# Retention outputs copied out of their PSUM bank by ScalarE, their squares summed in place, their transposes in the same bank

## The chip, the core and the metric

The kernel runs on one core of a Trainium2 chip. The core has TensorE (PE, matrix products, with a loader of its own for weights, PEld), VectorE (DVE), ScalarE (ACT), GpSimd (POOL) and SyncE (SP, which here issues DMAs); each works through its own queue in order, and they wait for each other by semaphores. PE writes into PSUM, eight banks of 2 KB per partition, which the other engines read; everything else is in SBUF. The metric is the device time of one execution in microseconds (us).

## The reference, cut to what matters

A trunk of two layers. In each, one projection of the modulated input feeds three token mixers and a gate; the mixer that the change touches is the bidirectional retention: four heads of width 64, ten chunks (tiles) of 128 tokens, eight of the latent tokens and two of the context.

```python
def step(s, inp):
    qi, ki, vi = inp
    a = jnp.einsum('bihd,bjhd->bhij', qi, ki) * intra
    o = (jnp.einsum('bhij,bjhe->bihe', a, vi)
         + jnp.einsum('bihd,bhde->bihe', qi, s) * q_dec[None, :, :, None])
    ...
def bidir_retention(q, k, v, log_g, s0_f, s0_b):
    ...
    o = rms_norm(o_f + jnp.flip(o_b, 1))   # over the 64 of each head
    return o.reshape(B, L, RET_W).astype(v.dtype), ...
# then: concat(o_ret, o_gqa, o_mla) * silu(z_gate), one output projection, residual add
```

## The kernel before

The layer's gate projection is computed output group by output group (z_blk, four calls, 24 matmuls per PSUM bank: L683 to L685, the operands split in a high and a low part; ScalarE takes a tanh, L688, VectorE multiplies it into a tile eo, L690, 256 columns each, and SP stores it, L691). Between halves of these groups z_blk takes one step of a side generator, `more` (L693), which runs in turn: key transposes, latents, the retention (retention, driver loop from L919), and last the preparation of the attention, which puts its key, value and kpr loads into SP's queue (L1086, L1101 to L1104, L1090, L1144) and their splits onto ScalarE and VectorE (L196, L197, L1147). So PE has gate matmuls to do while the short chains of the retention pass from engine to engine. The program's scheduler merges these into one fixed order per engine, by its own estimates; nothing in the code fixes it.

The retention goes over its ten tiles in a pipeline of four stages; step t of the driver loop does stage c of tile t-2, stage b of tile t-1 and stage a of tile t.

- Stage a: q is transposed (PE, L868, four) and k (L871, two) into two "tp" banks; VectorE scales q (qdT, L875), ScalarE writes q into a block-diagonal tile BD (L877, L878) and k into kT (L880); GpSimd advances a state (L825, L826). The transposes of stage d of tile t-3 are called from here and write into the free half of k's bank.
- Stage b: two products of BD and kT (PE, L893), masked by VectorE into At (L895).
- Stage c: eight matmuls (PE, L903 and L904) write the tile's output into one half of the bank "o"; ScalarE squares it into the other half (L905), VectorE sums the squares per head (L907), takes the inverse root in 13 small operations (newton, L145 to L161) and multiplies the output by it from PSUM into the SBUF tile oret (L910).
- Stage d: two transposes of oret (PE, L916) and ScalarE's copy to the mixer's result yx (L917).

Of the kind "o" there is one bank at that time, so the first L903 of a tile waits until L910 of the tile before has read it. Of the kind "acc" there are five: the gate groups and the attention's scores (L1247, L1248; maximum by VectorE, L1256; exponential with its sum by ScalarE, L1270) take turns in them. In the attention 128 queries against 512 keys are one score tile.

Of the kernel before, what the change touches and what calls it, by code (L numbers as in the profile page):

```python
# [10 lines left out]
F32 = mybir.dt.float32  # L11
F32R = mybir.dt.float32r
I32 = mybir.dt.int32
AF = mybir.ActivationFunctionType
ALU = mybir.AluOpType
AX = mybir.AxisListType
PSUM = bass.MemoryType.PSUM

P = 128
# [62 lines left out]
def hybrid_trunk(tc, I, O):  # L82
# [3 lines left out]
    V, A, G, T = nc.vector, nc.scalar, nc.gpsimd, nc.tensor  # L86
# [47 lines left out]
    def bank(tag):  # L134
        if tag == "o":
            return pp.tile([P, 512], F32, name=tag, tag=tag, bufs=1)
        if tag == "m":
            tag = "tp"
        bufs = {"acc": NACC, "tp": 7 - NACC}[tag]
        return pp.tile([P, 512], F32, name=tag, tag=tag, bufs=bufs)  # L140
# [647 lines left out]
    def retention(l, rt, load, kv):  # L788


        dec, cdec = dec_all[:, l], cdec_all[:, l]
        MT = rt.tile([P, 4, 128], F32, name="MT")
        dma(MT.rearrange("p h c -> p (h c)"), s_mt[l])
        pos = rt.tile([P, 256], F32, name="pos", tag="cur", bufs=2)[:, 0:128]
        dma(pos[0:64, :], I["rel"][0:1, 0, :].to_broadcast([64, 128]))
        dma(pos[64:128, :], I["rel"][127:128, 1, :].to_broadcast([64, 128]))

        def bc(ap, lo=0, hi=P):
            return ap.unsqueeze(2).to_broadcast([hi - lo, 4, 64])

        def h4(ap):
            return ap.rearrange("p (h d) -> p h d", h=4)

        F, B = slice(0, 64), slice(64, 128)
        S = rt.tile([P, NT, 256], F32, name="S")
        fin = rt.tile([P, 256], F32, name="fin")
        for d, t in ((F, 0), (B, NL - 1)):
            dma(h4(S[d, t, :]), I["state_ret"][0, l, d.start // 64].rearrange("h d e -> d h e"))
        V.memset(S[F, NL, :], 0.0)
        V.memset(S[B, NT - 1, :], 0.0)  # L810


        decT = rt.tile([P, 4, 128], F32, name="decT")
        for h in range(4):
            lg = lgT_all[:, l, h:h + 1]
            A.activation(decT[:, h, :], pos, AF.Exp, scale=lg, bias=lg)

        def advanced(eng, d, nxt, cur, inc=None):

            if inc is not None:  # L820
                eng.tensor_tensor(h4(nxt), h4(cur), bc(cdec[d], d.start, d.stop), op=ALU.mult)
                eng.tensor_tensor(nxt, nxt, inc, op=ALU.add)
            else:
                st = rt.tile([P, 256], F32, name="cur", tag="cur", bufs=2)[d]
                pin(eng.tensor_tensor(h4(st), h4(cur), bc(cdec[d], d.start, d.stop), op=ALU.mult))  # L825
                eng.tensor_tensor(nxt, nxt, st, op=ALU.add)  # L826

        def increments(t, kv):
            kd = rt.tile([P, 4, 2, 64], F32, name="kd", tag="kd", bufs=3)
            V.tensor_tensor(kd, h4(kv[:, 0:256]).unsqueeze(2).to_broadcast([P, 4, 2, 64]),  # L830
                            dec[:, 2:4, :].rearrange("p a h -> p h a").unsqueeze(3).to_broadcast([P, 4, 2, 64]), op=ALU.mult)
            ps = bank("m")
            for h in range(4):
                T.matmul(ps[:, h * 64:(h + 1) * 64], kd[:, h, :, :].rearrange("p a b -> p (a b)"),
                         kv[:, 256 + h * 64:256 + (h + 1) * 64], start=True, stop=True)

            if t not in (0, NL, NT - 1):
                advanced(V, B, S[B, t - 1, :], S[B, t, :], ps[B, :256])
            elif t == NL:
                advanced(V, B, fin[B, :], S[B, t, :], ps[B, :256])  # L840
            elif t == NT - 1:
                V.tensor_copy(S[B, t - 1, :], ps[B, :256])

            if t != NL - 1:
                A.copy(S[F, t + 1, :] if t != NT - 1 else fin[F, :], ps[F, :256])

        qqs = {}

        def doubled(t):
            if t < NT:  # L850
                qqs[t] = rt.tile([P, 4, 2, 64], F32, name="qq", tag="kd", bufs=3)
                pin(pool_copy(qqs[t], h4(yx[t][:, 0:256]).unsqueeze(2).to_broadcast([P, 4, 2, 64])))

        for t in range(NT - 1, -1, -1):
            yield
            nx_kv = load(t - 1) if t else load(0)
            increments(t, kv)
            if t < 2:
                doubled(1 - t)
            kv = nx_kv  # L860

        BD = rt.tile([P, 2, 256], F32, name="BD")
        V.memset(BD, 0.0)

        def stage_a(t, kv, qq):
            pt = bank("tp")
            for h in range(4):
                T.transpose(pt[:, h * 128:(h + 1) * 128], qq[:, h, :, :].rearrange("p a b -> p (a b)"), ident)  # L868
            pk = bank("tp")
            for j in range(2):  # L870
                T.transpose(pk[:, j * 128:(j + 1) * 128], kv[:, j * 128:(j + 1) * 128], ident)  # L871
            if t >= 3:
                stage_d(t - 3, outs.pop(t - 3), pk[:, 256:512])
            qdT = rt.tile([P, 4, 128], F32, name="qdT", tag="qdT", bufs=2)
            V.tensor_tensor(qdT.rearrange("p h c -> p (h c)"), pt, decT.rearrange("p h c -> p (h c)"), op=ALU.mult)  # L875
            pq = pt.rearrange("p (j x c) -> p x j c", j=2, x=2)
            A.copy(BD[0:64, :, 0:128], pq[0:64, 0])  # L877
            A.copy(BD[64:128, :, 128:256], pq[64:128, 1])  # L878
            kT = rt.tile([P, 2, 128], F32, name="kT", tag="kT", bufs=1)
            A.copy(kT.rearrange("p j c -> p (j c)"), pk[:, 0:256])  # L880

            if t < NL - 1:
                advanced(G, F, S[F, t + 1, :], S[F, t, :])
            elif t == NL:
                advanced(G, F, fin[F, :], S[F, NT - 1, :])
                for d in range(2):
                    dma(new_state[0, l, d].rearrange("h d e -> d h e"), h4(fin[64 * d:64 * d + 64, :]))
            return kv, qdT, kT

        def stage_b(kT):  # L890
            pa = bank("m")
            for j in range(2):
                T.matmul(pa[:, j * 256:(j + 1) * 256], kT[:, j, :], BD[:, j, :], start=True, stop=True)  # L893
            At = rt.tile([P, 4, 128], F32, name="At", tag="kd", bufs=3)
            V.tensor_tensor(At.rearrange("p h c -> p (h c)"), pa, MT.rearrange("p h c -> p (h c)"), op=ALU.mult)  # L895
            return At

        def stage_c(t, kv, qdT, At):
            bo = bank("o")
            po, sq = bo[:, 0:256], bo[:, 256:512]  # L900
            for h in range(4):
                hs = slice(h * 64, (h + 1) * 64)
                T.matmul(po[:, hs], At[:, h, :], kv[:, 256 + h * 64:256 + (h + 1) * 64], start=True, stop=False)  # L903
                T.matmul(po[:, hs], qdT[:, h, :], S[:, t, hs], start=False, stop=True)  # L904
            A.activation(sq, po, AF.Square)  # L905
            ss = sm.tile([P, 4], F32, name="ss4", tag="ss4")
            V.tensor_reduce(ss, h4(sq), axis=AX.X, op=ALU.add)  # L907
            rstd = newton(ss, 4, 1.0 / 64)
            o = rt.tile([P, 256], F32, name="oret", tag="cur", bufs=2)
            V.tensor_tensor(h4(o), h4(po), bc(rstd), op=ALU.mult)  # L910
            return o

        def stage_d(t, o, pt):

            for i in range(2):
                T.transpose(pt[:, i * 128:(i + 1) * 128], o[:, i * 128:(i + 1) * 128], ident)  # L916
            A.copy(yx[t][:, 0:256], pt)  # L917

        st, At, outs = {}, {}, {}  # L919
        for t in range(NT + 3):  # L920
            yield
            if 2 <= t < NT + 2:
                outs[t - 2] = stage_c(t - 2, st[t - 2][0], st[t - 2][1], At.pop(t - 2))
            if 1 <= t <= NT:
                At[t - 1] = stage_b(st[t - 1][2])
            if t < NT:
                nx_kv = load(t + 1) if t + 1 < NT else None
                if t:
                    doubled(t + 1)
                st[t] = stage_a(t, kv, qqs.pop(t))  # L930
                kv = nx_kv
            elif t >= 3:
                stage_d(t - 3, outs.pop(t - 3), bank("tp")[:, :256])

    def cache_keys(l, pool, bufs):

# [581 lines left out]
    st, p1, acts = open_p1(ws)  # L1518
# [66 lines left out]
    for l in range(DEPTH):  # L1585
        ws = Weights(out_blocks(l) + (in_blocks(l + 1) if l + 1 < DEPTH else []))
        att.run(ws)
        st, p1, acts = open_p1(ws)
# [3 lines left out]
        ss, rstd = {}, {}  # L1592
# [100 lines left out]
```

## Time and profile before

| | us |
|---|---|
| runs of the kernel | 2162.13, 2163.22, 2165.7; median 2163.22 |
| profiled execution | 2162.85 |
| its span, first to last instruction | 2161.1 |
| PE busy | 2084.2 (96%) |
| VectorE busy | 1502.0 (70%) |
| ScalarE busy | 1183.5 (55%) |
| GpSimd busy | 978.2 (45%) |
| granted TensorE clock, mean | 0.992 |

In layer 0 the retention's L910 runs from 424.6 to 486.2 us of the span and the first scores come at 506.46; in layer 1 the last L910 runs at 1528.1. The attention follows each. In a timeline a row is one run of like instructions on one engine: its start, its length, the line, the tile written and read. What is in brackets is how long the engine was idle before, and what released it. Matmuls are pipelined, so what one costs PE is the distance between two starts, not its length.

### The profile page before, as it was taken

To read this page: it belongs to the slowest core of one execution; us is meant where nothing else is said; L and a number is where in the kernel's file an instruction comes from. 1 tells how busy PE (TensorE), PEld (TensorE's weight loads), DVE (VectorE), ACT (ScalarE), POOL (GpSimd) and SP (SyncE) were. 2 spreads that over 40 slices of the span, in tenths; PEclk is the share of its full clock that TensorE was granted. 3 is DMA by queue.
4 is the path that set the end of the run, shared out by engine and by line. 5 is a ranking of instruction groups with operands and counts; after the bars stand their busy time and mean duration, and the time that the engine had idled before them with its cause. 6 is when DMAs were issued, how large, how long until landed. Compare 5 with 4: busy or idle time off the path is not lost. (4 is left out here: it accounts for less than half of the span.)

```text
span 2161.1 us, 42292 instructions
## 1 busy us (share of the span) xinstructions
PE 2084.2 (96%) x14888; PEld 1870.0 (87%) x14888; DVE 1502.0 (70%) x3830; ACT 1183.5 (55%) x3180; POOL 978.2 (45%) x1444
## 2 busy tenths in 40 slices
PE   7999999999999999999999999998999999999998
PEld 3899987788888888888999999887788888888898
DVE  4625583666889999997174358546689899999824
ACT  3503333225788888886243233322488888888623
POOL 2341242315576465533543324233375656453474
PEclk8999999999999999999999999999999999999999
DMA  9542446414111010004143212452311111000322
GB/s 315 145 145 63 123 112 204 122 49 117 36 44 28 20 30 25 13 27 136 46 153 102 66 54 55 140 152 66 109 46 30 32 30 32 14 22 18 98 91 98
DMA packets 189117, 173.30 MB, mean 80 GB/s; under 512 B 35833, under 2 KB 171625, under 8 KB 188905
## 3 DMA queue, kind: packets, MB, share of 16 engines
q1 hardware_dynamic: 187464, 165.35, 25.7%
q10 hardware_dynamic: 1440, 5.24, 0.6%
q8 instruction: 119, 1.95, 0.4%
q14 instruction: 94, 0.76, 0.1%
HBM read 124.77 MB, written 45.76 MB: 79 GB/s over the span
## 5 line engine op out<-in xcount | busy, mean ns | idle before, releaser
L256 PE MATMUL acc<-wh,ah 128*128 128x256 f32 (+1 forms) x1760 | 503.4, 286 | 1.8 <-ACT ah L404 1.8
L258 PE MATMUL acc<-wh,al 128*128 128x256 f32 (+1 forms) x1760 | 500.6, 284 | 2.5 <-DVE al L405 2.4
L257 PE MATMUL acc<-wl,ah 128*128 128x256 f32 (+1 forms) x1760 | 502.7, 286 | 0.0
L1256 DVE TENSOR_REDUCE nm<-acc 128x1 f32<-128x512 f32 (+1 forms) x624 | 411.7, 665 | 39.0 <-PE acc L1250 27.0
L1293 DVE TENSOR_TENSOR pT<-tp,pT 128x512 fp32r<-128x512 f32 (+1 forms) x624 | 413.2, 664 | 36.1 <-ACT pT L1292 30.6
L1292 ACT CAST pT<-tp 128x512 fp32r<-128x512 f32 (+1 forms) x624 | 356.5, 573 | 139.1 <-PE tp L1288 132.8
L1270 ACT ACTIVATE pn<-acc,nm 128x512 f32<-128x512 f32 (+1 forms) x624 | 421.3, 681 | 19.9 <-DVE nm L1261 17.4
L1288 PE MATMUL tp<-ident,pn 128*128 128x128 f32 x2400 | 424.1, 274 | 3.9 <-DVE pT L1293 2.4
L256 PEld LDWEIGHTS acc<-wh,ah 128*128 128x128 f32 x1760 | 334.9, 190 | 13.1 <-issue 8.2
L258 PEld LDWEIGHTS acc<-wh,al 128*128 128x128 f32 x1760 | 332.0, 189 | 5.3 <-DVE al L405 4.5
L257 PEld LDWEIGHTS acc<-wl,ah 128*128 128x128 f32 x1760 | 334.0, 190 | 0.8 <-issue 0.8
L1304 PE MATMUL o<-pT,V 128*128 128x256 f32 x1200 | 326.3, 294 | 0.7 <-DVE yx L1317 0.6
L1288 PEld LDWEIGHTS tp<-ident,pn 128*128 128x128 f32 x2400 | 287.6, 140 | 34.6 <-PE tp L1288 5.8
L1305 PE MATMUL o<-pT,V 128*128 128x256 f32 x1200 | 314.4, 284 | 0.0
L1304 PEld LDWEIGHTS o<-pT,V 128*128 128x128 f32 x1200 | 227.1, 189 | 19.2 <-DVE yx L1317 5.1
L1305 PEld LDWEIGHTS o<-pT,V 128*128 128x128 f32 x1200 | 227.2, 189 | 16.6
L192 POOL TENSOR_SCALAR wh<-raw 128x512 fp32r<-128x512 f32 (+2 forms) x144 | 82.4, 582 | 321.2 <-PE acc L258 143.2
L193 POOL TENSOR_TENSOR wl<-raw,wh 128x512 fp32r<-128x512 f32 (+2 forms) x144 | 164.7, 1155 | 5.2
L1247 PE MATMUL acc<-K,Qm 128*128 128x512 f32 (+1 forms) x312 | 140.6, 451 | 1.0
L683 PE MATMUL acc<-ah,wh 128*128 128x512 f32 (+1 forms) x384 | 141.4, 368 | 0.0
L684 PE MATMUL acc<-ah,wl 128*128 128x512 f32 (+1 forms) x384 | 139.8, 364 | 0.0
L685 PE MATMUL acc<-al,wh 128*128 128x512 f32 (+1 forms) x384 | 139.5, 363 | 0.0
(278 smaller groups left out, 3898.3 us busy)
## 6 DMA issues: line engine op xcount, KB each, us to landing
raw<-in_w_ada_dram SPq DMA_DIRECT2D x96, 256.0 KB, 3.2
raw<-in_w_in_dram SPq DMA_DIRECT2D x56, 256.0 KB, 2.9
kv<-s_rkv SPq DMA_DIRECT2D x40, 256.0 KB, 2.8
s_gT<-eo SPq DMA_DIRECT2D x80, 128.0 KB, 2.2
yx<-in_x_sample_dram SPq DMA_DIRECT2D x16, 512.0 KB, 6.4
gt<-s_gT SPq DMA_DIRECT2D x60, 128.0 KB, 2.1
raw<-in_w_in_dram SPq DMA_DIRECT2D x56, 128.0 KB, 2.5
raw<-in_w_out_dram SPq DMA_DIRECT2D x48, 128.0 KB, 3.0
```

Source lines behind the costliest of these rows:

```text
L193: G.tensor_tensor(wl, raw, wh.bitcast(F32), op=ALU.subtract)
L256: T.matmul(ps, ah[:, k, :], wh, start=(k == 0), stop=False)
L257: T.matmul(ps, ah[:, k, :], wl, start=False, stop=False)
L258: T.matmul(ps, al[:, k, :], wh, start=False, stop=(k == KC - 1))
L683: T.matmul(ps, wh, ah[:, k, :], start=(k == 0), stop=False)
L1256: V.tensor_reduce(nm[:, b:b + 1], ps, axis=AX.X, op=ALU.max, negate=True)
L1270: A.activation(pn, ps, AF.Exp, bias=p.ng[i], accum_out=p.su[:, i, b:b + 1])
L1288: T.transpose(pt[:, c * 128:(c + 1) * 128], pn[:, c * 128:(c + 1) * 128], ident)
L1292: A.copy(ph, p3)
L1293: V.tensor_tensor(pl, p3, ph.bitcast(F32), op=ALU.subtract)
L1304: T.matmul(p.po, vc, p.gran[b][:, 0, c, :], start=(ch == 0), stop=False)
L1305: T.matmul(p.po, vc, p.gran[b][:, 1, c, :], start=False, stop=(ch == last))
```

## The change

Stage c gets its bank from the driver loop. When the eight matmuls are done, ScalarE copies the output to oret at once, and then squares it head by head in place in the bank, each square writing its sum into one column of ss; newton works on ss as before, and VectorE multiplies oret by the result in place in SBUF. Stage d is called first in step t, ahead of stage c of tile t-2, and its transposes go into the other half of that step's bank "o" instead of the half of a "tp" bank; the last stage ds take no "tp" bank any more. Per layer ten reductions on VectorE go, and ten squares of 256 columns on ScalarE become ten copies and forty squares of 64 columns with sums. PE, GpSimd and SP have the same instructions as before.

```diff
@@ stage_a
-            if t >= 3:
-                stage_d(t - 3, outs.pop(t - 3), pk[:, 256:512])
...
@@ stage_c
-        def stage_c(t, kv, qdT, At):
-            bo = bank("o")
-            po, sq = bo[:, 0:256], bo[:, 256:512]
+        def stage_c(t, kv, qdT, At, po):
...
-            A.activation(sq, po, AF.Square)
+            o = rt.tile([P, 256], F32, name="oret", tag="cur", bufs=2)
+            A.copy(o, po)
             ss = sm.tile([P, 4], F32, name="ss4", tag="ss4")
-            V.tensor_reduce(ss, h4(sq), axis=AX.X, op=ALU.add)
+            for h in range(4):
+                hs = slice(h * 64, (h + 1) * 64)
+                A.activation(po[:, hs], po[:, hs], AF.Square, accum_out=ss[:, h:h + 1])
             rstd = newton(ss, 4, 1.0 / 64)
-            o = rt.tile([P, 256], F32, name="oret", tag="cur", bufs=2)
-            V.tensor_tensor(h4(o), h4(po), bc(rstd), op=ALU.mult)
+            V.tensor_tensor(h4(o), h4(o), bc(rstd), op=ALU.mult)
             return o
@@ driver loop
         for t in range(NT + 3):
             yield
+            if t >= 2:
+                bo = bank("o")
+            if t >= 3:
+                stage_d(t - 3, outs.pop(t - 3), bo[:, 256:512])
             if 2 <= t < NT + 2:
-                outs[t - 2] = stage_c(t - 2, st[t - 2][0], st[t - 2][1], At.pop(t - 2))
+                outs[t - 2] = stage_c(t - 2, st[t - 2][0], st[t - 2][1], At.pop(t - 2), bo[:, 0:256])
...
-            elif t >= 3:
-                stage_d(t - 3, outs.pop(t - 3), bank("tp")[:, :256])
```

In the changed kernel the lines are: matmuls of stage c L899 and L900, copy L902, squares L906, product L908, transposes of stage d L914, copy to yx L915; stage b L891, its product At L893, qdT L873, BD L875 and L876, kT L878.

The scheduler orders the instructions anew. PE in the loop, before; a tile's small matmuls stand close together (acc are the gate matmuls, ah and al the split operands):

```order
L893 MATMUL tp<-BD,kT 128x256 x2
L868 MATMUL tp<-ident,qq 128x128 x4
L683 MATMUL acc<-ah_129,wh 128x512
L903 MATMUL o<-kv,At 128x64
L904 MATMUL o<-S,qdT 128x64
...
L871 MATMUL tp<-ident,kv 128x128 x2
L916 MATMUL tp<-ident,oret 128x128 x2
```

PE in the loop, after; eight gate matmuls follow stage c, then come stage b and stage a, and some 21 gate matmuls stand in a step where before some 11 did:

```order
L914 MATMUL o<-ident,oret 128x128 x2
L685 MATMUL acc<-al_132,wh 128x256
L683 MATMUL acc<-ah_127,wh 128x512
L684 MATMUL acc<-ah_127,wl 128x512
L899 MATMUL o<-kv,At 128x64
L900 MATMUL o<-S,qdT 128x64
...
L685 MATMUL acc<-al_128,wh 128x512
L683 MATMUL acc<-ah_127,wh 128x512
```

The last stage d has moved from ahead of the layer's remaining gate groups to just ahead of the attention's first scores. ScalarE in the loop, after (th is the gate's tanh):

```order
L915 COPY yx<-o 128x256
L688 ACTIVATE th<-acc 128x256
L902 COPY oret<-o 128x256
L906 ACTIVATE o,ss_5830<-o 128x64 x2
L875 COPY BD<-tp 64x2x128
L906 ACTIVATE o,ss_5830<-o 128x64
L876 COPY BD<-tp 64x2x128
L906 ACTIVATE o,ss_5830<-o 128x64
L878 COPY kT<-tp 128x256
```

Three of the four squares now stand ahead of the second BD copy. PE at the end of the retention, after; behind the last stage d stand the first scores:

```order
L683 MATMUL acc<-ah_127,wh 128x512
L684 MATMUL acc<-ah_127,wl 128x512
L685 MATMUL acc<-al_128,wh 128x512
L914 MATMUL o<-ident,oret 128x128 x2
L1247 MATMUL acc<-K,Q_6422 128x512 x2
L1248 MATMUL acc<-K,Q_6422 128x512
L1247 MATMUL acc<-K,Q_6422 128x512
L683 MATMUL acc<-ah_129,wh 128x512
```

Before, 91 gate matmuls stood between the last L916 and the first L1247. SP there, before (st are the staging tiles of the loads):

```order
L691 DMA s_gT_58<-eo 128x256 x5
L1086 DMA st<-s_gkT_66 64x4x128 x3
L1086 DMA st<-s_gkT_66 64x2x128
L1101 DMA st<-in_cache_gqa_v_dram 128x4x64
L1102 DMA st<-s_kv_62 128x3x64
L1104 DMA st<-s_kv_62 128x7x64
L691 DMA s_gT_58<-eo 128x256 x2
L1090 DMA st<-s_mk_68 64x512 x3
```

SP there, after; the same loads stand behind six stores, and one store is left among them:

```order
L691 DMA s_gT_58<-eo 128x256 x6
L1086 DMA st<-s_gkT_66 64x4x128 x3
L691 DMA s_gT_58<-eo 128x256
L1086 DMA st<-s_gkT_66 64x2x128
L1101 DMA st<-in_cache_gqa_v_dram 128x4x64
L1102 DMA st<-s_kv_62 128x3x64
L1104 DMA st<-s_kv_62 128x7x64
L1090 DMA st<-s_mk_68 64x512 x3
```

VectorE there, after: the eo of the sixth store stands within the last newton, and the key splits (L197) follow the product:

```order
L159 TENSOR_TENSOR nwu<-nwu,nwx 128x4
L690 SCALAR_TENSOR_TENSOR eo<-th,acc 128x256
L160 SCALAR_TENSOR_TENSOR nwy<-nwu,nwy 128x4
L908 TENSOR_TENSOR oret<-oret,nwy 128x256
L690 SCALAR_TENSOR_TENSOR eo<-th,acc 128x256
L197 TENSOR_TENSOR K<-st,K 64x512 x3
L1256 TENSOR_REDUCE nm<-acc 128x1
```

Before, five evacuations and the first key splits alternated behind the last L910, with PE still in gate matmuls.

## Rows read from the trace of the kernel before

**Rows 1.** The page's first section: busy time, share of the span, instructions.

```profile
PE 2084.2 (96%) x14888; PEld 1870.0 (87%) x14888; DVE 1502.0 (70%) x3830; ACT 1183.5 (55%) x3180; POOL 978.2 (45%) x1444
```

**Rows 2.** Line L910 (last two: who waited, line waited at, us, times).

```profile
L910 DVE TENSOR_TENSOR oret<-o,nwy x20: 407/425/425, 424.6 to 1528.1; 128x256 f32<-128x256 f32 x20
...
  PE o L903: 9.3, 11
```

**Rows 3.** PE's timeline, layer 0: start, length, operation, [idle before <- releaser].

```profile
436.29 0.40 PE L683 MATMUL acc<-ah,wh 128*128 128x512 f32 x1
436.53 0.40 PE L684 MATMUL acc<-ah,wl 128*128 128x512 f32 x1
...
439.76 0.43 PE L903 MATMUL o<-kv,At 128*128 128x64 f32 x2 [1.07 <-DVE oret L910]
...
446.17 1.02 PE L893 MATMUL tp<-BD,kT 128*128 128x256 f32 x4
447.02 0.33 PE L903 MATMUL o<-kv,At 128*128 128x64 f32 x2
...
448.76 0.61 PE L868 MATMUL tp<-ident,qq 128*128 128x128 f32 x4
449.20 0.38 PE L871 MATMUL tp<-ident,kv 128*128 128x128 f32 x2
```

**Rows 4.** ScalarE's timeline, the same tiles.

```profile
449.02 0.37 ACT L905 ACTIVATE o<-o 128x256 f32<-128x256 f32 x1 [1.40 <-PE o L904]
...
471.55 0.37 ACT L877 COPY BD<-tp 64x256 f32<-64x256 f32 x1 [1.81 <-DVE nwu L151]
471.82 0.37 ACT L917 COPY yx<-tp 128x256 f32<-128x256 f32 x1
472.20 0.37 ACT L878 COPY BD<-tp 64x256 f32<-64x256 f32 x1
```

**Rows 5.** ScalarE's groups by form at L358: total and mean ns.

```profile
L358 ACT ACTIVATION_READ_ACCUMULATOR e<-acc 128x1 f32 x40 | 8.1, 202 | 0.0
...
L358 ACT ACTIVATE e<-acc 128x128 f32<-128x128 f32 x20 | 5.8, 288 | 0.0
```

**Rows 6.** VectorE's timeline, two tiles.

```profile
477.94 0.59 DVE L152 TENSOR_SCALAR nwy<-nwu 128x4 int32<-128x4 int32 x1
...
483.83 0.17 DVE L150 TENSOR_SCALAR nwx<-ss 128x4 f32<-128x4 f32 x1
...
486.21 0.42 DVE L910 TENSOR_TENSOR oret<-o,nwy 128x256 f32<-128x256 f32 x1
```

**Rows 7.** GpSimd's timeline behind the last tiles.

```profile
476.93 1.57 POOL L1171 TENSOR_TENSOR Q<-yx,Q 64x256 fp32r<-64x256 f32 x2
```

**Rows 8.** SP's queue, its loads for the attention: length is of all x.

```profile
488.20 4.81 SPq L1086 DMA_DIRECT2D st<-s_gkT  x4
...
501.52 8.96 SPq L1144 DMA_DIRECT2D st<-s_kpT  x16
```

**Rows 9.** ScalarE's timeline at the start of the attention.

```profile
491.07 0.62 ACT L196 CAST K<-st 64x512 fp32r<-64x512 f32 x1 [2.36 <-DMA st<-s_gkT]
...
513.97 0.40 ACT L1147 CAST kpr<-st 128x256 fp32r<-128x256 f32 x1
...
516.82 0.68 ACT L1270 ACTIVATE pn<-acc,nm 128x512 f32<-128x512 f32 x1
...
517.49 0.69 ACT L1270 ACTIVATE pn<-acc,nm 128x512 f32<-128x512 f32 x1
```

**Rows 10.** PE's timeline, the first and the fourth score tile.

```profile
506.46 0.86 PE L1247 MATMUL acc<-K,Q 128*128 128x512 f32 x3
...
517.16 0.47 PE L1247 MATMUL acc<-K,Q 128*128 128x512 f32 x1 [0.71 <-DVE eo L690]
```

**Rows 11.** The same stretch of layers 0 and 1: us, busy of engines, PEclk, DMA.

```profile
439.76:517.16 77.40, 74.22 (x431) 64.59 (x432) 46.91 (x152) 24.83 (x63) 17.89 (x28) 0.96 0.28 79
1482.17:1557.96 75.79, 71.60 (x431) 61.75 (x432) 46.59 (x152) 24.81 (x63) 17.95 (x28) 1.00 0.28 81
```

## The prediction

> **What bounds the kernel now.** I read the page's first section, then the waits of one line, then the timelines of one layer. TensorE (PE) is busy for 96% of the span [rows 1]: a change counts only where it makes PE wait or lets it stop waiting. So the question for the line that is replaced (L910, the product that reads the PSUM bank "o" last) is who waited for it: PE's first L903 of a tile, 9.3 us in 11 of the 20 tiles of both layers [rows 2]; PE's timeline shows one, 1.07 us before 439.76 [rows 3]. Those 9.3 us are all that an earlier copy can give back.
>
> The rest of the argument needs prices. PE goes from one 512-column matmul of the gate projection to the next in 0.235 us; the eight small matmuls of stage c take 1.74 (447.02 to 448.76), stage b 0.85 (446.17 to 447.02), the four transposes of q 0.44 (448.76 to 449.20) and so the two of k some 0.22 [rows 3]. On ScalarE the 256-column square begins 0.26 after PE has gone on from stage c (448.76, 449.02) and lasts 0.37; copies follow each other after 0.27 (64 partitions) and 0.38 [rows 3, 4]. On VectorE newton and L910 take 2.8 (483.83 to 486.21, plus 0.42), and each of newton's 13 operations waits for the one before [rows 6].
>
> **The change, part by part; per layer, ten tiles.**
>
> (1) *Removed: the wait for L910.* The bank is now read last by the fourth square, before newton begins. -9.3 / 2 = -4.65.
>
> (2) *Added on ScalarE: a copy and four squares with sums in place of one square.* A square of 64 columns is not in the trace. The nearest rows are 0.37 for 256 columns [rows 4] and 0.29 for 128 with its sum, whose read-out is 0.20 more [rows 5]: 64 columns give about 0.24. Of two exponentials one behind the other, the second starts 0.67 after the first, which lasts 0.68 itself [rows 9], so there the read-out costs nothing: a square costs 0.24 at the least and 0.44 at the most; I take 0.3. VectorE loses the reduction L907, 0.4 per tile, off PE's path.
>
> (3) *Moved: the loop's order.* After, a tile's chain stands in this order on PE: two transposes of the output (stage d), 3 gate matmuls, stage c, 8 gate matmuls, stage b, q's transposes, 2, k's transposes, 8, and the next stage d. That gives two places where PE may wait, in about 7 steady tiles.
> A hand-over between engines I set at 0.06, an estimate: newton's 13 operations of 0.17 fill 2.38 [rows 6], so one within VectorE is some 0.02, and I take three of these. Stage b needs both BD copies, and ScalarE now does the copy and three of the squares ahead of the second: 0.26 + 0.38 + 3 x 0.3 + 0.27 + 0.38 + 0.06 = 2.25 after stage c, against a cover of 8 x 0.235 = 1.88. Wait 0.37, with a square at 0.24 or 0.44 0.2 or 0.8: 7 x 0.37 = **2.6** (1.4 to 5.6).
> Stage d needs newton, which begins after the fourth square: 0.26 + 0.38 + 1.2 + 0.65 + 0.06, newton and product 2.8, and in between on VectorE the masked product At (512 columns from PSUM, so between L910's 0.42 and twice that: 0.6), and 0.06: 6.0. Each gate evacuation (eo, 256 columns from PSUM as L910, 0.42) that falls in it adds 0.4, none to two, 0.3 on average; a VectorE operation stretched beside GpSimd (L152 0.59 instead of 0.17 while L1171 runs) adds 0.4 [rows 6, 7], half of the time. So 6.5, against 18 x 0.235 + 0.85 + 0.44 + 0.22 + 0.37 (the wait before b) = 6.1. Wait 0.4: 7 x 0.4 = **2.8** (0 to 4).
> Stage c follows d after 3 matmuls and needs the yx copy, since d and c share the bank: 0.26 + 0.38 + 0.06 against 0.14 + 0.70, so nothing (at most 0.1 each). Before, d wrote into the half of k's bank that was free, and its copy kept nobody waiting.
> The multiply's input is now SBUF twice (L908), where L910 had one in PSUM and took 407 to 425 ns in all 20 tiles [rows 2]; I price it the same. The Trainium skill, "SBUF — State Buffer", section "Who interferes with whom", says that a VectorE instruction with two SBUF inputs contends with a GpSimd instruction that reads SBUF, and that the loser blocks. By that rule L908 can lose what the stretched row shows, 0.42 in each of 20 tiles: up to 8.4 more, 2202; it stands beside the worse rival and not in the sum.
>
> (4) *The last tile.* Behind the last stage c the program now has 13 gate matmuls, 3.05, and then the last stage d; nothing else is left of the layer's retention to fill in. Its chain: 0.26 + 0.38 + 1.2 + 0.06 + 2.8 + 0.4 (an eo that now stands within that newton) + 0.06 = 5.2, so a wait of 2.1 (1.8 to 2.7), and more if GpSimd's q pieces (L1169, L1171), which ran right behind the last tiles before, stretch two to five of the small operations by 0.42 each: 0.9 to 2.1. I take **3.7** (1.8 to 4.8).
>
> (5) *The attention's first keys.* Before, SP issued the key loads (L1086) at 488.20 and PE came to the first score matmul at 506.46, 18 us later, without a wait [rows 8, 10]. After, those loads stand in SP's queue behind the store of the eo that lies in the last newton, about 0.2 us before PE's last d, and the score matmuls stand right behind d. From issue to the cast on ScalarE 2.87, the cast 0.62 and a subtraction on VectorE of about its size: 4.2 [rows 8, 9]; less 0.34 for d and the head start, less some slack in the estimate: **3.7** (3.2 to 4.2).
>
> (6) *The sixth score tile.* There are five "acc" banks; the sixth tile needs one that an exponential has freed, and the first exponential stands on ScalarE behind the four kpr casts, the last of 27 loads on SP. Counted from the first load's issue: 16 kpr loads took 8.96, 0.56 each [rows 8], so 27 without a stop are 15.1; landing up to 2.9, cast 0.4, exponential 0.6: 19.0 at the least. Before, with stores and their waits in between, the last kpr load was out at 510.48, 22.3 after the first: 26.2 at the most. The order after has one store among the 27 where before had four, but the casts have to keep their buffers free: 22.5. PE gets there after 4.2, ten score matmuls and 24 gate matmuls at 0.235 and 24 of half width: 4.2 + 8.0 + 2.9 + 0.7 (its present wait for an eo at the fourth tile, 517.16 [rows 10]) = 15.8. Wait **6.7** (3.2 to 10.4). Before, the same casts were done at 514.37 and the exponentials could begin when the scores came (516.82) [rows 9].
>
> *Sum per layer:* -4.65 + 2.6 + 2.8 + 3.7 + 3.7 + 6.7 = 14.85; two layers 29.7. *The clock:* layer 0's granted clock was 0.96 over its retention and layer 1's 1.00; the same stretch was 1.6 longer in layer 0 [rows 11]. With longer waits I expect about the same loss in each layer, 3.0 in all instead of 1.6: +1.4 (-1.6 to +3). The profiled run took 2162.85; 2162.85 + 31.1 = 2194.0, and the median of the runs is 0.4 above it, which is inside the rounding: 2194.
>
> **Rivals.**
> *Faster.* Only (1) comes true: stage b and d are covered, the key loads are out at least 10 us before the last d because the scheduler's queue order leaves SP free, and the clock stays up: -9.3 - 1.6, 2152. For it: the bank really is released some 3 us earlier. Against: the order of the rows shows the score matmuls behind d and the loads behind that eo; SP cannot pass the store. Chance 0.05.
> *Same.* The delay is given back in the attention, where PE would then wait less for exponentials: 2163. Against: PE is 96% busy over the span, with few gaps to take it up [rows 1], and the stages behind start when PE gets to them. Chance 0.04.
> *Worse than forecast.* In steps b and d the high ends hold: squares at 0.44 and VectorE blocked by GpSimd in every tile (0.42 for L908 or a newton step): +3.0 and +2.9 per layer, and the sixth tile late by another 4. 2194 + 2 x 9.9 = 2214. For it: the 0.59 of L152 in the row; against: only a few of newton's operations are stretched now. The rule of the page that I named would add to this. Chance 0.11.
> *The forecast*, 0.80.
>
> **How the numbers follow.** Low ends of every term: -4.65 + 1.4 + 0 + 1.8 + 3.2 + 3.2 = 4.95 per layer, 9.9, less 1.6 of the clock: 2171. High ends: -4.65 + 5.6 + 4 + 4.8 + 4.2 + 10.4 = 24.4, 48.7, plus 3: 2214.5. Not all ends come at once, so 2172 to 2214 holds the forecast's case and half of the worse one; the faster and the same case lie outside. A measurement of this kernel can tell 0.2%, 4.3 us, from no change. Faster by more 0.05, within 0.04, slower 0.91.
>
> **What would show it.** In the changed kernel's waits of PE: none for the output's copy or squares at the first matmul of stage c beyond 0.1; L891 waiting for ScalarE's BD copies and L914 for L908, both below 1 us in the steady tiles; L914 of the last tile 2 us or more; the first L1247 behind a DMA or the K subtraction 3 to 4 us, and a later L1247 behind an exponential 3 to 10 us, in both layers alike. In ScalarE's timeline a square with its read-out of 0.24 to 0.44. I am wrong if those two waits at the start of the attention are small (the loads were early after all), or if they are there and the stretch from there to the layer's end is shorter by as much.

## The result and the profile after

The changed kernel takes 2210.78 us (median of four runs, 2207.81 to 2212.83), the kernel before 2162.68 beside it: a ratio of 1.0219, 95% interval 1.0201 to 1.0236, slower by 48 us. The forecast was 2194, range 2172 to 2214: slower as forecast and inside the range, 17 us above its middle. The profiled execution took 2211.14.

The page of the changed kernel, its busy times; they answer to [rows 1]:

```profile
PE 2102.7 (95%) x14888; PEld 1875.6 (85%) x14888; DVE 1489.5 (67%) x3810; ACT 1209.1 (55%) x3340; POOL 976.2 (44%) x1444
```

PE has the same 14888 instructions and is busy for 18.5 us more (2102.7 against 2084.2). The waits of PE in the whole execution (us in total, times, longest), first of the kernel after, then two of the kernel before:

```profile
PE tp L1358 <- POOL rb L1355: 16.1, 6, 5.1
PE acc L1247 <- ACT pn L1270: 11.7, 2, 6.0
PE o L914 <- DVE oret L908: 11.0, 14, 3.4
PE acc L1247 <- DVE K L197: 8.0, 4, 3.8
...
PE tp L891 <- ACT BD L876: 2.0, 11, 0.4
```

```profile
PE tp L1358 <- POOL rb L1355: 9.9, 6, 3.2
...
PE acc L1247 <- ACT pn L1270: 1.3, 2, 0.7
```

The wait of [rows 2], 9.3 us at the first matmul of stage c, is gone from the list: the change did what it says. In its place stand L914, stage d behind newton, 11.0; the first keys, 8.0; the sixth score tile behind its exponential, 11.7 where there were 1.3; and L1358, a transposition in the attention behind GpSimd, 16.1 where there were 9.9. What changed is 10.4 + 10.7 (L916, stage d before, waited 0.3) + 8.0 + 1.7 (stage b before 0.3) + 6.2 - 9.3 = 27.7 of the 48.3 us between the two spans (2209.4 and 2161.1).

The end of layer 0's retention on PE, after; it answers to [rows 3, 10]:

```profile
508.74 0.41 PE L914 MATMUL o<-ident,oret 128*128 128x128 f32 x2 [3.44 <-DVE oret L908]
512.90 0.77 PE L1247 MATMUL acc<-K,Q 128*128 128x512 f32 x1 [3.75 <-DVE K L197]
...
515.39 0.63 PE L683 MATMUL acc<-ah,wh 128*128 128x512 f32 x1
515.82 0.63 PE L684 MATMUL acc<-ah,wl 128*128 128x512 f32 x1
...
532.59 0.79 PE L1247 MATMUL acc<-K,Q 128*128 128x512 f32 x1 [5.74 <-ACT pn L1270]
```

All three waits stand where they were looked for: 3.44 for the last newton, 3.75 for the first key, 5.74 at the sixth tile. Between them PE goes from one gate matmul to the next in 0.43 (515.39 to 515.82), where it took 0.235 in [rows 3]. The same is seen in the granted clock (the number ahead of the last two), columns as in [rows 11]:

```profile
510.00:520.00 10.00, 6.82 (x21) 5.18 (x22) 6.20 (x11) 3.98 (x7) 3.04 (x5) 0.66 0.44 116
530.00:540.00 10.00, 6.71 (x25) 4.96 (x26) 6.10 (x14) 6.96 (x18) 5.37 (x8) 0.66 0.64 171
580.00:590.00 10.00, 6.36 (x31) 5.96 (x32) 3.28 (x7) 2.53 (x8) 8.04 (x14) 0.66 0.03 7
```

A mean of 0.66 in 10 us is some 6.8 us at half speed, the lower of the two levels, 1.2 GHz. In the kernel before the same stretches stood at 1.00; 440 to 450 was one of two in layer 0's retention that stood lower, at 0.83, half as long:

```profile
440.00:450.00 10.00, 10.00 (x63) 9.04 (x63) 6.34 (x22) 2.89 (x9) 2.03 (x4) 0.83 0.19 44
```

Not all of this time is work. After the change the clock is at half speed from 510.1 on, while PE still waits for the first key, and the part behind 512.90 alone slows matmuls (the first busy time is PE's):

```profile
510.10:512.90 2.80, 0.00 (x0) 0.03 (x1) 0.97 (x2) 1.49 (x3) 2.50 (x5) 0.50 0.55 168
512.90:516.90 4.00, 3.72 (x8) 2.64 (x9) 2.70 (x4) 0.84 (x3) 0.44 (x1) 0.50 0.43 101
```

Over the whole execution the mean granted clock fell from 0.992 to 0.984:

```profile
core 0: 2209.4 us, clock 0.984
```

(1 - 0.984) x 2209.4 is 35.4 us of full speed not granted, (1 - 0.992) x 2161.1 is 17.3: 18 us more, part of which fell on time in which PE waited anyway. In all stretches at half speed together PE was busy for 51.4 us after the change and for 26.6 before; half of that, 25.7 and 13.3 us, is what the slow clock cost its work: 12.4 us more. So the 48.3 us are 29.8 of idle time (27.7 of them the waits above) and 18.5 of busy time, 12.4 of these the clock. Of the other 6, most is time that the list of waits leaves out, as (3) shows further down.

Further rows of after. ScalarE's first two squares in the last tile, and SP's queue at the start of the attention; they answer to [rows 4, 5] and to [rows 8]:

```profile
502.67 0.21 ACT L906 ACTIVATE o<-o 128x64 f32<-128x64 f32 x1
...
503.02 0.21 ACT L906 ACTIVATE o<-o 128x64 f32<-128x64 f32 x1
```

```profile
487.69 20.64 SPq L691 DMA_DIRECT2D s_gT<-eo  x6
508.39 2.00 SPq L1086 DMA_DIRECT2D st<-s_gkT  x3
...
522.65 7.45 SPq L1144 DMA_DIRECT2D st<-s_kpT  x16
```

A square of 64 columns lasts 0.21, and the next begins 0.35 after the first has begun. SP waits in its six stores from 487.69 on and issues the first key load at 508.39, 0.35 ahead of the last stage d.

### The profile page after: what moved, and what is told of

Its sections match the earlier page's. It is cut to its first block, busy times and chain, and to the rows that moved or that the text cites. A ratio compares the mean times of both kernels' runs of the same rounds, so it can differ in the third digit from the quotient of the medians.

```text
span 2209.4 us, 42399 instructions
## 1 busy us (share of the span) xinstructions
PE 2102.7 (95%) x14888; PEld 1875.6 (85%) x14888; DVE 1489.5 (67%) x3810; ACT 1209.1 (55%) x3340; POOL 976.2 (44%) x1444
## 4 chain that ended last, share of the span: by engine, by line
PE 66%; DVE 5%; POOL 4%; ACT 4%; issue 2%; DMA 2%; SPq 0%; POOLq 0%; DVEq 0%; ACTq 0%
PE tp L1288 11%; PE o L1304 6%; PE acc L1247 6%; PE acc L257 6%; PE acc L258 6%; PE acc L256 6%; PE o L1305 6%; PE acc L1248 5%; PE acc L1250 3%; PE acc L685 2%; PE acc L683 2%; PE acc L684 2%; ACT o L906 1%; PE o L900 1%; PE o L899 1%
## 5 line engine op out<-in xcount | busy, mean ns | idle before, releaser
L1247 PE MATMUL acc<-K,Qm 128*128 128x512 f32 (+1 forms) x312 | 141.2, 453 | 1.0
L1248 PE MATMUL acc<-K,Qm 128*128 128x512 f32 (+1 forms) x312 | 139.7, 448 | 0.0
```

The costliest lines, as they stand in the source:

```text
L1247: T.matmul(ps, p.Q[:, 0, qs], K, start=True, stop=False)
L1248: T.matmul(ps, p.Q[:, 1, qs], K, start=False, stop=not p.mla)
```

## Experiments: the order of stage c and stage d

Theory 1 was formed from the order of the rows. In the changed kernel stage d of a tile stands on PE ahead of stage c of the next, and d waits for its tile's newton. So copy, squares, newton, product, d, the yx copy and c make one chain from tile to tile, and that the bank is released early is of no use. In this kernel only ScalarE and VectorE read PSUM, and after the change ScalarE alone reads the output's half of the bank. Theory 2 was that ScalarE's and VectorE's new work is the cause, theory 3 that the shared bank is.

**e1: stage c first, then stage d.**

```diff
             if t >= 2:
                 bo = bank("o")
-            if t >= 3:
-                stage_d(t - 3, outs.pop(t - 3), bo[:, 256:512])
             if 2 <= t < NT + 2:
                 outs[t - 2] = stage_c(t - 2, ..., bo[:, 0:256])
+            if t >= 3:
+                stage_d(t - 3, outs.pop(t - 3), bo[:, 256:512])
```

> The changed kernel with one thing swapped: in a step of the loop the eight matmuls of stage c come first and the transposes of stage d behind them, still in the same bank. Theory 1 (the order d before c is the cause: c of one tile stands on PE behind d of the tile before, which waits for that tile's newton, so copy, squares, newton, d and the yx copy form one chain from tile to tile, the retention takes 21 gate matmuls per step, ends late and leaves nothing between the last d and the scores): the steps shrink to some 14 gate matmuls, PE waits for nothing longer than 1 us at the scores, 2150 to 2165. Theory 2 (what ScalarE and VectorE got, the copy, forty squares and a product with two SBUF inputs, is the cause): hardly better than the changed kernel, 2195 to 2211. Theory 3 (the shared bank is the cause): 2195 to 2211 as well, since it is still shared.

Measured: 2155.92, ratio to the kernel before 0.9962 (0.9947 to 0.9977). In the profile of e1 PE does not wait for the bank at stage c, the waits for the first keys are gone, and the rest is as before the change:

```profile
PE tp L1358 <- POOL rb L1355: 9.6, 6, 3.1
...
PE acc L1247 <- DVE eo L690: 1.8, 2, 1.0
...
PE o L914 <- DVE oret L908: 1.0, 2, 0.5
```

From one L914 to the next it takes 6.7 us (445.85 to 452.53) where the changed kernel takes 9.1 (444.55 to 453.62), and 41 + 24 + 24 gate matmuls stand between the last d and the scores, where the changed kernel has none: what fills its longer steps is missing there. First e1, then the changed kernel:

```profile
445.85 0.44 PE L914 MATMUL o<-ident,oret 128*128 128x128 f32 x2
...
452.53 0.44 PE L914 MATMUL o<-ident,oret 128*128 128x128 f32 x2
```

```profile
444.55 0.41 PE L914 MATMUL o<-ident,oret 128*128 128x128 f32 x2 [0.26 <-DVE oret L908]
...
453.62 0.41 PE L914 MATMUL o<-ident,oret 128*128 128x128 f32 x2 [0.24 <-DVE oret L908]
```

Even with its longer steps the changed kernel waits for the product at d, so the chain really takes that long. Two lines in another order are worth 55 us. Everything that theories 2 and 3 blame is still in e1.

**e2: the copy at once, stage d where it was before.**

```diff
-            if t >= 2:
-                bo = bank("o")
-            if t >= 3:
-                stage_d(t - 3, outs.pop(t - 3), bo[:, 256:512])
...
+            # in stage_a, as before
+            if t >= 3:
+                stage_d(t - 3, outs.pop(t - 3), pk[:, 256:512])
```

> Only the first half of the change: the copy at once, the squares in place and the product in SBUF; stage d is where it was before, in k's bank. Theory 1 (order) : the waits of stage c for the product go (9.3 us in the profile of the kernel before) and nothing comes late, 2150 to 2160. Theory 2 (ScalarE's and VectorE's new work): 2195 to 2211. Theory 3 (shared bank): 2150 to 2160, and 30 us or more below e1.

Measured: 2154.91, ratio 0.9962 (0.9949 to 0.9975), the same as e1. So the shared bank costs nothing where c comes first, with squares of this length (e10 below doubles them), and the first half of the change alone is a gain of some 8 us, which is about what [rows 2] showed as the wait for L910.

**e3: the kernel before, only stage d moved to the start of the step.**

```diff
             yield
+            if t >= 3:
+                stage_d(t - 3, outs.pop(t - 3), bank("tp")[:, :256])
             if 2 <= t < NT + 2:
                 outs[t - 2] = stage_c(t - 2, st[t - 2][0], st[t - 2][1], At.pop(t - 2))
```

> The kernel before, with its one square, reduction and product from PSUM, where only stage d is moved to the start of a step, ahead of stage c, into a bank of its own of the kind tp. Theory 1 (order): stage c stands behind d, d behind newton; the steps become some 18 gate matmuls long and PE waits for L910 at d instead of at c; some slack is left behind the last d (13 gate matmuls of 512, 24 of 256, 24 of 512 columns), so the scores are not late: 2160 to 2180. Theories 2 and 3: as the kernel before, 2161 to 2165.

Measured: 2170.91, ratio 1.0038 (1.0023 to 1.0053): slower than before by 8, as theory 1 has it, without any of the new work of ScalarE. PE waits for the product at d now, and at the scores for an evacuation:

```profile
PE acc L1245 <- DVE eo L690: 9.9, 2, 5.0
...
PE tp L914 <- DVE oret L908: 6.1, 13, 0.9
```

**e4: the changed kernel with one square and one reduction.**

```diff
-            for h in range(4):
-                hs = slice(h * 64, (h + 1) * 64)
-                A.activation(po[:, hs], po[:, hs], AF.Square, accum_out=ss[:, h:h + 1])
+            A.activation(po, po, AF.Square)
+            V.tensor_reduce(ss, h4(po), axis=AX.X, op=ALU.add)
```

> The changed kernel with one square of 256 columns in place and one reduction on VectorE instead of four squares with sums. Theory 1 (order): the chain from tile to tile is still there but some 0.6 us shorter per tile, the last d stands 23 gate matmuls ahead of the scores, so the key loads are out earlier: 2165 to 2195. Theory 2 in the narrow form (the four squares with their read-outs are the cause): 2150 to 2165.

Measured: 2190.13, ratio 1.0123 (1.0106 to 1.014). The chain is still there and shorter: 8.3 from one L913 (stage d here) to the next, where the changed kernel takes 9.1. The last d of layer 0 comes at 498.08 instead of 508.74. That is worth 21 us of the 48: the last d now has 23 gate matmuls behind it, the first key comes in time, and of the three waits at the end only that of the sixth tile is left.

```profile
PE acc L1246 <- ACT pn L1269: 13.7, 2, 6.9
```

So the length of the chain counts, but because of the order.

## Experiments: the waits at the attention and the clock

**e5: PE kept at work in two of the waits.**

```diff
+            if t == NT + 2:
+                for _ in range(30):
+                    T.transpose(bo[:, 0:128], ident, ident)
             if t >= 3:
                 stage_d(t - 3, outs.pop(t - 3), bo[:, 256:512])
+            if t == NT + 2:
+                for _ in range(28):
+                    T.transpose(bo[:, 0:128], ident, ident)
```

> The changed kernel with 30 transposes of the identity, which nobody reads, on PE ahead of each layer's last stage d and 28 behind it, into the free half of that bank: 3.3 and 3.1 us of work in place of the two waits of 3.4 and 4.0 us, so that PE is not idle there. Theory A (the time behind is set by the loads on SP, through the kpr casts and the first exponential): the half-clock stretch behind the first scores goes, but the 2 us that it cost come back as a longer wait of the sixth score tile: 2206 to 2213. Theory B (each wait carries the price of the slow clock behind it, which adds to the total): some 4 to 7 us less, 2203 to 2207.

Measured: 2203.99, ratio 1.0193 (1.0174 to 1.0211), 6.8 less than the changed kernel by the medians, though PE does 116 transposes more. The two did not run side by side, and the intervals of their ratios overlap a little (1.0201 to 1.0236). The two waits are gone from PE's list. The sixth tile and the clock:

```profile
PE acc L1253 <- ACT pn L1276: 14.8, 2, 7.6
```

```profile
510.92 0.39 PE L1253 MATMUL acc<-K,Q 128*128 128x512 f32 x1
511.15 0.40 PE L1254 MATMUL acc<-K,Q 128*128 128x512 f32 x1
```

```profile
core 0: 2202.2 us, clock 0.987
```

The first scores now go 0.23 apart (510.92, 511.15) instead of 0.42 to 0.6 in the changed kernel, and the sixth tile waits 1.6 us longer per layer, as theory A had it; but the total fell as theory B had it. By the mean clocks, (1 - 0.987) x 2202.2 = 28.6 us not granted against 35.4, so 6.8 less. PE's busy time shows it too: 2108.9 us, some 2096.3 without the transposes (3.34 and 2.98 per layer), against 2102.7, so 6.4 less. That is the size of the gain; it isn't proof, since the last d also came 2.2 us earlier in layer 0 (506.49 against 508.74), 0.9 of it in the loop.

**e6: four kpr loads instead of sixteen.**

```diff
-                for j in range(4):
-                    dma(st[32 * j:32 * j + 32, :n].rearrange("p (t c) -> p t c", c=P), src[...])
+                dma(st[:, :n], s_mk[l][0:128, ks])
```

> The changed kernel with the 16 kpr loads ahead of the attention replaced by four loads of as many bytes into the same tiles (they fetch rows of another tensor, so the rotary part of the scores is computed from wrong keys). Theory A (27 loads in SP's queue set the sixth tile): the last kpr cast comes about 12 x 0.46 = 5.5 us earlier, the sixth tile's wait falls from 5.9 to about 1, the half-clock stretch behind it goes, GpSimd's value splits and with them the waits at L1358 come back by some us too: 2185 to 2198. Rival (the maxima on VectorE, or the keys' splits, are as late): 2205 to 2211.

Measured: 2202.03, ratio 1.0194 (1.0171 to 1.0217), 8.8 less than the changed kernel, which again did not run beside it; the expectation was 13 to 26, so theory A fell short, and its rival's 2205 to 2211 was missed as well. The wait fell by half, from 11.7 to 5.5, and L1358 hardly:

```profile
PE tp L1357 <- POOL rb L1354: 15.7, 6, 4.3
...
PE acc L1246 <- ACT pn L1269: 5.5, 2, 2.9
```

SP's queue in e6 shows what was overlooked: with fewer loads it is not busy, it waits. The key, value and kpr loads go through three staging tiles, and a load is issued when VectorE has split the one that lay there:

```profile
522.45 0.34 SPq L1143 DMA_DIRECT2D st<-s_mk  x1
...
524.64 1.22 SPq L1143 DMA_DIRECT2D st<-s_mk  x2
```

```profile
SPq L1143 <- DVE K L197: 2.2, 3, 1.3
```

So the number of the loads is about half of what the sixth tile waits for. That the other half is the round of staging, cast and split is read from SP's waits and was not tried by itself.

**e7: e5 and e6 together.**

> e5 and e6 together: the four loads and the two fillings, so that no wait of some us is left idle at the end of the retention. Theory A: with the loads out of the way the two us of the slow clock behind the first scores are gained for good: 3 to 7 us below e6. If the clock costs nothing there: as e6 within 2 us.

Measured: 2192.41, ratio 1.0144 (1.0126 to 1.0163), 9.6 below e6, which ran beside it; theory A had 3 to 7. The mean clock is 0.991, almost that of before, and L1358 waits 9.9 us as before the change:

```profile
core 0: 2187.6 us, clock 0.991
```

```profile
PE tp L1363 <- POOL rb L1360: 9.9, 5, 3.0
PE acc L1252 <- ACT pn L1275: 8.2, 3, 4.1
```

(1 - 0.986) x 2199.7 = 30.8 against 19.7: 11 us that were not granted come back, for 10 us of time. That alone would not show that the clock made the gain, since L1358's waits fell by 5.8 as well. PE's busy time tells them apart: 2105.0 in e7, some 2092.4 without the transposes, against 2102.0 in e6. So the same work took PE 9.6 less, near what the means say. The profiled executions lie 12.1 apart; the other 3 or so are 5.8 less at L1358 and 14.7 less in the waits that were filled, against 12.6 of transposes and 4.4 more at the scores. Why L1358 returns only when both are done is open: its rows are made by GpSimd, which in the changed kernel began its first value split at 533.08 instead of 515.57, 17.5 later, when PE was 15 later; that its lateness there is the cause was read from the timelines and not tried by itself.

## Experiments: do the squares cost anything once the order is right?

**e8: e1 with one square and one reduction** (the edit of e4 in e1).

> e1 (stage c ahead of stage d) with one square of 256 columns in place and one reduction on VectorE instead of the four squares with sums. If the chain from tile to tile is really off PE's path in e1, it makes no difference how long the squares take: as e1, 2150 to 2160. If the squares still count there: 3 us or more away from e1.

Measured: 2146.07, ratio 0.993 (0.9911 to 0.995), 10 below e1, which had run at another time on another chip. By the expectation the squares would count; but a gain of 10 us has no place in the profile, where each retention, from the first matmul of stage c to the first scores, is 0.8 us shorter than e1's (82.9 against 83.7), and the rest lies in stages that have the same instructions. So it was tried again.

**e9: e2 with one square and one reduction.**

> e2 (stage d where it was before, copy at once) with one square of 256 columns and one reduction instead of the four squares with sums. If the 10 us between e1 and e8 belong to the squares, this lies some 8 to 10 us below e2's 2155: 2143 to 2149. If they belong to those two executions and not to the squares: 2150 to 2158.

Measured: 2150.47, ratio 0.9946 (0.9933 to 0.9958): 4.4 below e2, inside the second range by 0.5, so not clear by itself.

**e11 and e12: e1 and e8 again, side by side.**

> e1 again, beside e8 again on the same chip: 2152 to 2158 as before.

> e8 again, beside e1 again on the same chip. If the squares make the difference: 2144 to 2149, and 6 us or more below e11. If not: within 3 us of e11.

Measured: e11 2151.21, ratio 0.9954 (0.9941 to 0.9966); e12 2150.05, ratio 0.9946 (0.9933 to 0.996). e11 lies 0.8 below its range. Side by side the two are 1.2 us apart with intervals that lie over each other: four squares or one, no difference that five runs of each can tell. So the 10 us between e8 and e1, which ran at different times on different chips, did not come back; the intervals of their ratios (0.9911 to 0.995, 0.9947 to 0.9977) just overlap. e1, e2, e8, e9 and the two repetitions all lie below the kernel before, by 0.4 to 0.7%.

**e10: e1 with every square done twice.**

```diff
-            for h in range(4):
-                hs = slice(h * 64, (h + 1) * 64)
-                A.activation(po[:, hs], po[:, hs], AF.Square, accum_out=ss[:, h:h + 1])
+            for h in range(8):
+                hs = slice(h % 4 * 64, (h % 4 + 1) * 64)
+                A.activation(po[:, hs], o[:, hs], AF.Square, accum_out=ss[:, h % 4:h % 4 + 1])
```

> e1 with every square done twice (eight squares with sums per tile, of the copy in SBUF, into the bank): the cost of the squares doubled. If four squares cost e1 10 us, eight cost another 10 or more: 2165 to 2175. If they are off PE's path: 2150 to 2160. By the order the program's last d still has 24, 24 and 24 gate matmuls ahead of the scores, so nothing comes late there.

Measured: 2168.33, ratio 1.0032 (1.0019 to 1.0045), 17 above e11. Four squares are covered, eight are not: d, whose bank the squares are written to, now waits until the last of them is done, and the scores wait for evacuations. That nothing would come late there, as expected, did not hold. So with longer squares the shared bank does cost time.

```profile
PE acc L1247 <- DVE eo L690: 10.4, 4, 3.1
...
PE o L914 <- ACT o L906: 4.7, 10, 0.5
```

## Why the prediction was right, point by point

| step, us per layer | forecast | measured, layer 0 and layer 1 (waits as listed) |
|---|---|---|
| (1) wait for L910 | -4.65 | -4.3 and -5.0 (gone) |
| (3) stage b for BD | +2.6 | 0.8 and 1.2; from start to start 2.1 and 2.1 |
| (3) stage d in the loop | +2.8 | 2.2 and 2.0; from start to start 3.6 and 3.0 |
| (4) last stage d | +3.7 | 3.44 and 3.4 |
| (5) first key | +3.7 | 4.0 and 4.0 |
| (6) sixth tile | +6.7 | 5.7 and 6.0, less 0.7 before |
| clock, both layers | +1.4 | 12 |
| L1358 in the attention, both layers | none | +6.2 |

- **(1), (4) and (5)** were right in place and size, and (6) in place, 1.5 too large: the first exponential was to be done 22.5 after the first load's issue and was done after 24.1 (508.39 to 531.77, and 0.68), but PE came to the tile later as well, 18.5 after it instead of 15.8, 2 of that because it went at half speed behind the first scores. The four kpr casts stood ahead of it as said, the last at 531.46. In (6) the loads' number was named as the cause; e6 showed that it is about half of it.
- **(3), the prices on ScalarE.** A square was set at 0.3 (0.24 to 0.44); one followed by a square takes 0.35, one followed by a BD copy 0.21 or 0.33. The chain of stage b, set at 2.25, took 2.26 (447.22 to 449.48 in the fence). The cover was a little longer than 1.88, since the first gate matmul behind stage c takes 0.32, not 0.235. The wait is listed as 0.15 where 0.37 was forecast, but the two are counted differently: the list begins at the modelled end of the matmul before (448.93 and 0.40), the forecast where the next would have started (448.93 and 0.235). From start to start PE lost 0.31. Counted so over all tiles of a layer that follow a gate matmul, and less what the kernel before lost there, stage b took 2.1 and 2.1 and stage d in the loop 3.6 and 3.0: 5.7 and 5.1 against 5.4 forecast. So the loop's price was right.

```profile
447.22 0.48 PE L685 MATMUL acc<-al,wh 128*128 128x512 f32 x1
...
448.93 0.40 PE L683 MATMUL acc<-ah,wh 128*128 128x512 f32 x1
449.48 0.70 PE L891 MATMUL tp<-BD,kT 128*128 128x256 f32 x2 [0.15 <-ACT BD L876]
```

- **The product in SBUF.** It took 415 to 426 ns in all 20 tiles (columns as in [rows 2]):

```profile
L908 DVE TENSOR_TENSOR oret<-oret,nwy x20: 415/425/426, 424.8 to 1572.6; 128x256 f32<-128x256 f32 x20
```

By the rule of the Trainium skill that was weighed against it, "SBUF — State Buffer", section "Who interferes with whom", L908 and a GpSimd instruction that reads SBUF contend. The prediction worked out up to 0.42 more per tile for it, 2202. L908 lost nothing, but this is a thin test: GpSimd was at work beside it in only two of the 20 tiles, the last of each layer. In that of layer 0 L908 began at 508.17, and the GpSimd pair L1169 that ran then took 1.13 instead of 0.88; newton's small operations were stretched in the same tile, L160 to 0.58. In that the trace agrees with the rule: the two engines hold each other up. That L908 held up L1169 is read from the times and was not tried by itself. For this term the sum that left it out was right.

```profile
506.28 0.58 DVE L160 SCALAR_TENSOR_TENSOR nwy<-nwu,nwy 128x4 f32<-128x4 f32 x1
...
508.17 0.42 DVE L908 TENSOR_TENSOR oret<-oret,nwy 128x256 f32<-128x256 f32 x1
```

```profile
505.16 0.88 POOL L1169 TENSOR_SCALAR Qg<-yx 64x256 fp32r<-64x256 f32 x2 [0.57 <-PE acc L684]
...
507.73 1.13 POOL L1169 TENSOR_SCALAR Qg<-yx 64x256 fp32r<-64x256 f32 x2
```

- **The clock** is the step that was mis-sized. "I expect about the same loss in each layer, 3.0 in all instead of 1.6" priced three long waits per layer like the waits of 1 us before. The rows show two stretches of some 6.8 us at half speed at the start of the attention, and a third behind L1358, where layer 0 had three of half that length before; over the execution the slow clock cost PE's work 12.4 us more, not 1.4. e7, which takes the idle time away and not the work, got some 10 us back with the clock. [rows 11] held one term of this, the loss of a layer with such short stretches; what a wait of 4 to 6 us does to the clock was in no row of before that the sum used. There was such a row, at the start of the kernel: around a wait of 3.7 us before 48.62 (L387) the clock stood lower for 6.8 us in all.

```profile
40.00:50.00 10.00, 5.32 (x31) 3.71 (x31) 4.68 (x17) 7.33 (x20) 2.67 (x5) 0.80 0.99 358
50.00:60.00 10.00, 9.77 (x73) 8.52 (x72) 8.17 (x19) 9.31 (x25) 2.00 (x2) 0.86 0.70 223
```

- **The rival "same"** had the delay given back in the attention. The attention took 6 us more instead, at L1358; the forecast had no term for that, and its cause stays open (e7).
- **The sum** without the clock and L1358 was 29.7 against 22 by the listed waits (11.0 per layer), and the list counts (3) short by some 5. What it lacked is 11 us of clock and the 6.2 of L1358, together the 17 us by which the time lies above the middle. Without L1358's 6.2 and the clock's 12.4, 29.7 of the 48.3 us are left, the very sum; that it comes out so exactly is luck, since (6) was 1.5 too large per layer. The range's upper end, 2214, was made of the high ends of other terms; that it holds these 17 us as well is in part luck.
- **What the prediction did not name** is why all of this comes about. It took the new order (21 gate matmuls per step, d ahead of c) as given and counted the waits in it. That d ahead of c closes the chain from tile to tile, and that an early release of the bank can't help then, could have been read from the same rows, and e1 and e3 show it: the order alone costs the kernel before 8 us, and turning it round in the changed kernel wins 55.

## What to carry to other kernels

Before a bank is released earlier, look at what stands next on the engine that waits for it: if that is another step of the item before (here its transposes, which need the very result that the bank no longer waits for), the chain has only changed its last link and become longer. Call the step that continues the next item first, and the late step of the item before behind it; here that was two lines and 55 us. And price a wait on PE with the slow stretch behind it: here the slow clock cost PE's work 12 us on top of 28 us of waits.

## What was not expected of the hardware

Around waits of 3.4 to 6 us PE's granted clock stood at half for some 6.8 us (mean 0.66 in 10 us), 2 to 3 of them still in the wait and 4 to 5 in the work behind it; around the waits of 1.1 us of the kernel before it was half as long (0.83). Putting transposes of no use into two such waits per layer made the kernel faster: by 9.6 us beside the same kernel without them (e7 and e6), by 6.8 where the two did not run side by side (e5). And two programs whose medians were 10 us apart when they ran at different times on different chips (2155.9 and 2146.1) were 1.2 apart side by side: a difference of 0.3 to 0.5% between variants needs them side by side, and a repetition.
